# A hybrid decoder block: all eight gate pairs by seven block products, operand sums behind the last head's betas, gate and LayerNorm sums by accumulating transfers

## The chip, the core and the metric

The kernel runs on one core of a Trainium2 chip. The metric is the device time of one execution in microseconds; the time before is the median of three runs.

## What is computed

One layer of a decoder block on a sequence of 1024 tokens with 1024 channels, in float32. The part that matters here, cut from the reference:

```python
mod = c_act @ ada_w[l] + ada_b[l]
sh1, sc1, ga1, sh2, sc2, ga2 = [m[:, None, :] for m in jnp.split(mod, 6, axis=-1)]
h = rmsnorm(x, pre_mix_g[l]) * (1.0 + sc1) + sh1
...
proj = h @ w_in                                   # 1024 -> 1024 (GLU) + 1536 (q, k, v) + 2048 (gates)
glu_in, qkv, gates = jnp.split(proj, [...], axis=-1)
u_val, u_gate = jnp.split(glu_in, 2, axis=-1)
u = causal_depthwise_conv(u_val * jax.nn.sigmoid(u_gate), conv_w, conv_b)   # 512 channels, 31 taps
u = jax.nn.silu(layernorm(u, conv_ln_g, conv_ln_b))
y_conv = u @ w_conv_out
o = stick_breaking_attention(q, k, v)             # 8 heads of 64
y_att = o.reshape(b, s, ATT_WIDTH) @ w_att_out
g_conv, g_att = jnp.split(gates, 2, axis=-1)
merged = jax.nn.sigmoid(g_conv) * y_conv + jax.nn.sigmoid(g_att) * y_att
y = merged @ w_o
x = x + ga1 * rmsnorm(y, post_mix_g[l])
...                                               # then a SwiGLU feed-forward sub-layer of 2816 columns
```

## The kernel before

Channels lie on the 128 partitions and tokens on the free dimension, in two chunks of CH = 512. Each float32 operand of a large product is split into a high and a low part of TensorE's faster float32 form (tiles ending in hi and lo), and a product of 128 x 128 by 128 x 512 is three matmuls: hi by hi, hi by lo, lo by hi. The high part is a copy on ACT (line 143), the low part a subtraction on DVE (line 446 in the gate part, line 153 for whole weights).

The program runs in stages: the norm of x with its modulation (to about 67 us), then attention in four pairs of heads, with GLU and convolution as filler for TensorE, then the gates, the LayerNorm of the convolution, the projections of the two branches (pyc for the convolution, pya for attention), w_o (pwo), the feed-forward part and the final sums. The order of instructions on each engine is set by a scheduler at build time, from priorities, dependencies and how many buffers a tile name has; each engine then runs its own list in order and waits by semaphores. `load` issues a DMA on SP's queue, `store` on POOL's, and a few are issued on ACT's.

In attention a head's `be` tiles (betas) are multiplied on DVE (line 623), transposed by TensorE (`tr`), split into `ahi`/`alo` or, on the diagonal, `dhi`/`dlo` (lines 642 and 643), and multiplied with v (`av`). `pcv` are the products of the convolution, whose weights `cvw` come through SP's queue.

The 2048 gate columns are 16 tiles, taken as 8 pairs. For a pair in `GPAIRS`, the 2 x 2 block product of its weights with h is made from seven block products of 12 matmuls each instead of eight. Two of them (`early`, operands B11 and B21, results in the PSUM tile k, stored to e_d0 and s_d) run ahead, while the other operands aren't there yet; the weights for them are `ew`, split into `a`. The other five (`other_five`) use sums T1 to T4 of blocks of h, made from stored rows of x (`f`, from xm_d) for j = 0 to 3, and sums s1 to s4 of the weight blocks (`gs`), and leave their results in two PSUM tiles, ka and kc. `ga`, `gv`, `gw` are the tiles in which a pair's results are summed on DVE; after a sigmoid they are stored to s_d by POOL. The pairs not in `GPAIRS` (with NPL = 1 it is pair 7) are plain products: `gemm` into the tile pg, 96 matmuls for the pair.

`ln_all` is the LayerNorm of the convolution's four channel tiles `cr`: for each chunk the sum over the four is made in `la`, summed over partitions by a matmul with ones (`lnm`), subtracted, squared, summed again (`lnv`), and turned into a factor (`rstd_from`, lines 135 to 139) with which each `cr` is multiplied (line 851). The two chunks share the tiles `la` and `lm`. Then each `cr` gets gain, bias and swish (line 868), is split, and feeds pyc.

Of the kernel before, what the change touches and what calls it, by code (L numbers as in the profile page):

```python
# [17 lines left out]
P = 128  # L18
D = 1024
# [18 lines left out]
LATER = 100000  # L38
NPL = 1
GORDER = (0, 1, 2, 3, 4, 5, 6, 7)  # L40
# [29 lines left out]
def tile_block(ctx: ExitStack, tc: tile.TileContext, xT, vecs, ada1, ada2, win, wv, wcv, wat, wo, w1, w2, cvw, out):  # L70
# [378 lines left out]
    def prod0(bank_, w, b, first=True):  # L449
        for j in range(HK):  # L450
# [7 lines left out]
            for s, (st, mv) in enumerate(((0, 0), (0, 1), (1, 0))):  # L458
                pe.matmul(bank_, w[st][:, cols], mvs[mv], start=(first and j == 0 and s == 0),  # L459
                          stop=(j == HK - 1 and s == 2), skip_group_check=not first)  # L460

    with ExitStack() as sC:
        pc = mkpool(sC, "pc")
        with ExitStack() as sA:
            pa = mkpool(sA, "pa")
            psz = mkpool(sA, "psz", 2, space=PSUM)
            pst = mkpool(sA, "pst", 2, space=PSUM)
            ident = pa.tile([P, P], F32, name="ident")
# [10 lines left out]
            ndiag = count()  # L479

            def glu(ct):
# [99 lines left out]
            def head(p, hh, qst, kst, klo, vts, oT):  # L581
# [6 lines left out]
                for ci, c in enumerate(order):  # L588
# [5 lines left out]
                    for sc in range(nsc - 1, -1, -1):  # L594
                        probs = []
                        for i in (2 * c, 2 * c + 1):
# [26 lines left out]
                            dve.tensor_tensor(beta[:, :m], beta[:, :m], kap[:, s_lo + 1:s_lo + 1 + m], op=ALU.mult)  # L623
                            probs.append(beta)
# [30 lines left out]
            def attend(p, qk, vts):  # L655
                qs, ks, kl = qk
                oT = pa.tile([P, T], F32, tag="oT", name=f"oT{p}", bufs=1)
                nxt = None
                for hh in range(2):
                    with tc.high_priority(offset=SOONER):  # L660
                        head(p, hh, qs[hh], ks[hh], kl[hh], vts, oT)
                    if hh == 0 and p < 3:
                        nxt = qk_pair(p + 1)
                with tc.high_priority(offset=SOONER):
                    load(o_d[p], oT)
                return nxt
# [7 lines left out]
            for p in range(4):  # L674
# [5 lines left out]
                qk = attend(p, qk, v)  # L680
            conv(3)
            for n in PLAIN:
                gb = banks2(f"pg{n}")
# [32 lines left out]
    with ExitStack() as sG:  # L716
        pg = mkpool(sG, "pg")
        psg = mkpool(sG, "psg", 4, space=PSUM)

        def ot(name, dt=F32):  # L720
            return pg.tile([P, 2, CH], dt, tag="op", name=name, bufs=16)

# [15 lines left out]

        def make_t(name, src, hi_eng, lo_eng):
            t = ot(name, F32R)  # L740
            copy_to(hi_eng, t[:, 0], src)
            lo_eng.tensor_tensor(t[:, 1], src, t[:, 0], op=ALU.subtract)
            return t

        dsh1 = small.tile([P, HK], F32, name="dsh1")
        dve.tensor_tensor(dsh1, mod[:, HK:KT], mod[:, 0:HK], op=ALU.subtract)
        for j in range(HK):
            if j == 0:
                f = [pg.tile([P, T], F32, tag="f", name=f"f{q}_{j}", bufs=2) for q in range(2)]
                b11, b12, b21, b22 = f[0][:, :CH], f[0][:, CH:], f[1][:, :CH], f[1][:, CH:]  # L750
            else:
                b12, b11, b22, b21 = ((xt, st, xt)[j - 1](f"f{q}_{j}") for q in range(4))
            for b, k, c in ((b12, j, 1), (b11, j, 0), (b22, HK + j, 1), (b21, HK + j, 0)):
                load(b, xm_d[k][:, c * CH:(c + 1) * CH])
            sh, ds = mod[:, HK + j:HK + j + 1], dsh1[:, j:j + 1]
            dve.tensor_tensor(b11, b12, b11, op=ALU.subtract)
            dve.scalar_tensor_tensor(b12, b22, ds, b12, op0=ALU.add, op1=ALU.subtract)
            dve.scalar_tensor_tensor(b22, b22, sh, b11, op0=ALU.add, op1=ALU.subtract)
            dve.scalar_tensor_tensor(b21, b21, sh, b22, op0=ALU.add, op1=ALU.subtract)
            for b, src in (("T2", b22), ("T1", b11), ("T3", b12), ("T4", b21)):  # L760
                B0[b, j] = make_t(f"{b}o_{j}", src, act, dve)

        pairs, p1s, t3_done = {}, {}, []

        def pair_load(i):
# [5 lines left out]
            p1s[i] = xt(f"ga{i}")  # L771
            load(p1s[i], e_d0[i])

        def sig_out(t, n, c):
# [3 lines left out]
        def other_five(i):  # L778
            wg, wu = pairs[i]
            p1 = c21 = p1s[i]  # L780
            a11, a12, a21, a22 = wg[:, :CH], wg[:, CH:], wu[:, :CH], wu[:, CH:]
            s1, s2, s3 = (st(f"g{nm}_{i}") for nm in ("s1", "s2", "s3"))
            v, w_ = xt(f"gv_{i}"), xt(f"gw_{i}")
            dve.tensor_tensor(s1, a21, a22, op=ALU.add)
            dve.tensor_tensor(s2, s1, a11, op=ALU.subtract)
# [36 lines left out]
        def ln_all():  # L822
# [5 lines left out]
            for c in range(NCH):  # L828
                cs = hs[c]
                dve.tensor_tensor(s0_, cr[0][:, cs], cr[1][:, cs], op=ALU.add)  # L830
                for ct in (2, 3):
                    dve.tensor_tensor(s0_, s0_, cr[ct][:, cs], op=ALU.add)
                pm = psg.tile([P, CH], F32, tag="ln", name=f"lnm{c}", bufs=1)
# [42 lines left out]
        def ada2_dots(ins, n):  # L876
            for _ in range(n):
                col = a2.popleft()
                w = pg.tile([P, D], F32, tag="f", name=f"ada2_{col}", bufs=2)
                load(w, ada2[col - 2 * KT])  # L880
                with tc.issue_after(ins.ins):
                    dot_c(w, cb, col)
# [1079 lines left out]
```

## Time and profile before

| | |
|---|---|
| median of 3 runs | 1385.55 us (1385.22 to 1388.72) |
| profiled execution | 1385.58 us, span 1383.8 us, granted clock 1.00 |
| TensorE busy | 1369.8 us, 99% of the span, 6844 records |
| VectorE busy | 1041.5 us, 75%, 1593 instructions |
| ScalarE busy | 655.2 us, 47%, 1163 instructions |
| GpSimd busy | 108.8 us, 8%, 251 instructions |
| plain products of pair 7 (pg) | first at 392.0 us |
| early products (k) | 415.7 to 453.9 us |
| gate stage, first product of the other five | 453.9 us |
| first product with w_conv_out (pyc) | 551.4 us |

Times in a row of the profile are microseconds from the span's start, unless they are marked ns. A row names the line of the code, the engine, the operation, the output and the inputs by the program's names, and shapes. A bracket behind a row gives how long the engine had been idle before it and what ended the wait. Matmuls overlap, so that the time from one start to the next, not the duration of one, is what a matmul costs.

### The profile page before, as it was taken

How to read it: one execution, taken by the hardware profiler on the slowest of the kernel's cores; microseconds unless marked ns; L12 is line 12 of the kernel's file. 1: busy time of each engine (PE TensorE's matmuls, PEld its weight loads, DVE VectorE, ACT ScalarE, POOL GpSimd, SP SyncE). 2: the span in 40 equal slices, each digit the busy share in tenths (PEclk: the TensorE clock that was granted, in tenths of full speed). 3: DMA queues.
4: the chain of work that ended last, by engine and by line, in shares of the span. 5: the costliest groups of instructions: out<-in, count | busy, mean ns of one | idle time of the engine just before them, and what ended most of it. 6: DMA issues, size and time to landing. Idle time of an engine off the chain costs nothing.

```text
span 1383.8 us, 18854 instructions
## 1 busy us (share of the span) xinstructions
PE 1369.8 (99%) x6844; PEld 1154.7 (83%) x6844; DVE 1041.5 (75%) x1593; ACT 655.2 (47%) x1163; POOL 108.8 (8%) x251
## 2 busy tenths in 40 slices
PE   8999999999999999999999999999999999999998
PEld 6898888998988788887887888888888888888887
DVE  7997786675857888777597987778877775884354
ACT  6565564464646547313365543324444443434442
POOL 0100001000000011000012200001111110000002
PEclk9999999999999999999999999999999999999999
DMA  9512051140468547855745544457777779596736
GB/s 379 231 39 69 16 167 47 46 138 31 138 205 295 215 148 276 276 183 166 298 137 193 203 148 171 145 191 249 245 242 252 254 262 385 177 337 221 251 113 122
DMA packets 94941, 265.03 MB, mean 192 GB/s; under 512 B 10048, under 2 KB 21440, under 8 KB 93824
## 3 DMA queue, kind: packets, MB, share of 16 engines
q1 hardware_dynamic: 74080, 201.42, 43.2%
q0 software_dynamic: 17904, 57.42, 11.9%
q10 hardware_dynamic: 2864, 4.98, 1.0%
q8 instruction: 54, 0.88, 0.3%
q14 instruction: 39, 0.32, 0.1%
HBM read 192.74 MB, written 71.04 MB: 191 GB/s over the span
## 4 chain that ended last, share of the span: by engine, by line
PE 82%; DMA 5%; issue 5%; DVE 4%; ACT 2%; POOL 1%; SPq 0%; DVEq 0%; POOLq 0%; ACTq 0%
PE ka L1082 15%; PE kc L1082 8%; PE ka L1629 8%; PE pwo L1000 6%; PE ke L1191 4%; PE pb L1629 4%; PE pgv L164 3%; PE k L459 3%; PE pv L538 3%; PE pgg L164 2%; PE pk L164 2%; DMA ada<-in_ada_dram 2%; PE pcv L517 2%; PE pq L164 2%; PE tr L636 2%
## 5 line engine op out<-in xcount | busy, mean ns | idle before, releaser
L612 ACT ACTIVATE ka<-z 128x128 f32<-128x128 f32 (+2 forms) x96 | 47.2, 494 | 44.4 <-PE z L611 35.2
L1629 PE MATMUL ka<-gt,w2f 128*128 128x512 f32 x264 | 63.4, 389 | 0.0
L618 DVE TENSOR_TENSOR_SCAN ka<-ka,eye 128x128 f32<-128x128 f32 (+1 forms) x64 | 51.4, 815 | 11.9 <-ACT ka L612 11.8
L623 DVE TENSOR_TENSOR be<-be,ka 128x127 f32<-128x127 f32 (+2 forms) x96 | 53.8, 573 | 7.1 <-ACT be L614 2.0
L1629 PEld LDWEIGHTS ka<-gt,w2f 128*128 128x128 f32 x264 | 49.5, 188 | 10.3
L119 DVE SCALAR_TENSOR_TENSOR ada<-ada,cb 128x1024 f32<-128x1024 f32 x32 | 39.1, 1224 | 25.2 <-DMA ada<-in_ada_dram 25.0
L614 ACT ACTIVATE be<-z 128x127 f32<-128x127 f32 (+2 forms) x96 | 47.0, 496 | 6.0 <-PE tr L636 5.8
L636 PE MATMUL tr<-ident,be 128*128 128x128 f32 x288 | 46.5, 272 | 0.4 <-DVE be L623 0.4
L1191 PE MATMUL ke<-b,w_hi 128*128 128x512 f32 x176 | 44.3, 394 | 0.0
L621 DVE TENSOR_TENSOR_SCAN ka<-ka 128x512 f32<-128x512 f32 x32 | 40.6, 1275 | 3.7 <-ACT ka L612 3.6
L517 PE MATMUL pcv<-ph,cvw 128*128 128x128 f32 x320 | 42.9, 275 | 0.0
L642 ACT ACTIVATE ahi<-tr 128x512 fp32r<-128x512 f32 x48 | 28.3, 601 | 27.6 <-PE tr L636 19.4
L517 PEld LDWEIGHTS pcv<-ph,cvw 128*128 128x128 f32 x320 | 40.4, 191 | 0.7
L1191 PEld LDWEIGHTS ke<-b,w_hi 128*128 128x128 f32 x176 | 33.0, 188 | 7.7 <-issue 1.0
L143 ACT ACTIVATE gt<-X 128x512 fp32r<-128x512 f32 x33 | 20.3, 629 | 38.8 <-DVE X L1672 11.2
L643 DVE TENSOR_TENSOR alo<-tr,ahi 128x512 fp32r<-128x512 f32 x48 | 32.1, 685 | 7.9 <-ACT ahi L642 7.6
L636 PEld LDWEIGHTS tr<-ident,be 128*128 128x128 f32 x288 | 34.8, 140 | 3.8 <-PE z L611 0.7
L143 ACT ACTIVATE s1o<-s 128x512 fp32r<-128x512 f32 x22 | 13.8, 629 | 49.4 <-PE ka L1082 42.8
L538 PE MATMUL pv<-wv_hi,hhi 128*128 128x256 f32 x128 | 36.8, 288 | 0.2 <-DVE klo L578 0.2
L538 PE MATMUL pv<-wv_hi,hlo 128*128 128x256 f32 x128 | 36.6, 286 | 0.0
L538 PE MATMUL pv<-wv_lo,hhi 128*128 128x256 f32 x128 | 36.2, 284 | 0.0
L578 DVE TENSOR_TENSOR klo<-pk,kst 64x512 fp32r<-64x512 f32 x32 | 22.0, 689 | 18.7 <-ACT kst L575 18.3
(561 smaller groups left out, 4186.1 us busy)
## 6 DMA issues: line engine op xcount, KB each, us to landing
w_d<-w2o POOLq DMA_DIRECT2D x44, 512.0 KB, 7.4
w2f<-w_d SPq DMA_DIRECT2D x44, 512.0 KB, 4.7
ada<-in_ada_dram SPq DMA_DIRECT2D x32, 512.0 KB, 5.4
w2r<-in_w_dram SPq DMA_DIRECT2D x44, 256.0 KB, 3.8
w1g<-in_w_dram SPq DMA_DIRECT2D x21, 512.0 KB, 3.7
w1u<-in_w_dram SPq DMA_DIRECT2D x21, 512.0 KB, 6.0
cvw<-in_cvw_dram SPq DMA_DIRECT2D x20, 512.0 KB, 3.7
ada_w<-in_ada_dram SPq DMA_DIRECT2D x8, 1024.0 KB, 14.7
```

The costliest lines, as they stand in the source:

```text
L164: pe.matmul(bank, st[:, cols], mv[k][:, c * CH:(c + 1) * CH], start=(i == 0 and s == 0), stop=(i == n - 1 and s == 2))
L517: pe.matmul(cv[:, gi * TM:(gi + 1) * TM], wts[n][:, at:at + P], ph[:, g, SH - 1 - d:SH - 1 - d + TM], start=(d == 0), stop=(d == SH - 1))
L538: pe.matmul(pv[:, :256], st[k][:, tcols], mv[:, wc], start=(k == 0 and i == 0), stop=(k == KT - 1 and i == 2))
L612: act.activation(kap[:, s_lo:s_hi], z[:, zo:zo + w], AF.Sigmoid, bias=0.0, scale=-0.125)
L614: act.activation(beta[:, :m], z[:, zo:zo + m], AF.Sigmoid, bias=0.0, scale=0.125)
L618: dve.tensor_tensor_scan(rev, rev, eye[:, CH - w:][:, ::-1], 0.0, op0=ALU.mult, op1=ALU.add)
L623: dve.tensor_tensor(beta[:, :m], beta[:, :m], kap[:, s_lo + 1:s_lo + 1 + m], op=ALU.mult)
L636: pe.transpose(tr[:, o:o + P], probs[ii][:, jo:jo + P], ident)
L1000: pe.matmul(bank_, st[:, cols], mv[k][:, cs], start=(k == 0 and q == 0), stop=(k == KT - 1 and q == 2))
L1082: pe.matmul(bank_, st[:, cols], t[:, mv], start=(first and j == 0 and s == 0), stop=(j == HK - 1 and s == 2), skip_group_check=not first)
L1191: pe.matmul(kbs[f], wes[f][st][:, cols], t[:, mv], start=(i == 0 and j == 0 and st == 0 and mv == 0), stop=(j == HK - 1 and st == 1), skip ...
L1629: pe.matmul(dst, w[st][:, cols], g[mv], start=first and s == 0, stop=last and s == 2, skip_group_check=more)
```

## The change

1. `NPL = 0`: pair 7 is made by seven products like the others.
2. The operand sums (`t_ops`) of rows j = 0 and 1 are made at the end of attention, in tiles of the pool `pc` whose earlier contents (query, key, GLU and convolution tiles) are dead by then. Their first operation is ordered behind the last head's last multiplication of betas (`probs_at`), for the scheduler only. Rows 2 and 3 come later, as before. For this the pool `pc` lives on through the gate stage, the PSUM pools `psz` and `pst` live as long as `sC`, the T and Y operands get a list of places (`T_AT`, `Y_AT`), the tag "op" has 6 buffers instead of 16, and the later ada loads use the tag "ph".
3. The weight sum s1 = a21 + a22 of each pair is a load followed by an accumulating DMA on POOL's queue, instead of a sum on DVE.
4. The channel sum of the LayerNorm is, for each chunk, a load and three accumulating DMAs on POOL's queue, instead of three sums on DVE.
5. The last pair's attention output is stored by ACT's queue instead of SP's.

```diff
-NPL = 1
+NPL = 0
...
+    def t_ops(j, b11, b12, b21, b22, tiles, behind=None):
+        sh, ds = mod[:, HK + j:HK + j + 1], dsh1[:, j:j + 1]
+        t1 = dve.tensor_tensor(b11, b12, b11, op=ALU.subtract)
+        if behind:
+            tc.add_manual_dep(t1.ins, behind, ...SCHED_ONLY)
+        dve.scalar_tensor_tensor(b12, b22, ds, b12, op0=ALU.add, op1=ALU.subtract)
+        dve.scalar_tensor_tensor(b22, b22, sh, b11, op0=ALU.add, op1=ALU.subtract)
+        dve.scalar_tensor_tensor(b21, b21, sh, b22, op0=ALU.add, op1=ALU.subtract)
+        for b, src in (("T2", b22), ("T1", b11), ("T3", b12), ("T4", b21)):
+            t = tiles(f"{b}o_{j}")
+            copy_to(act, t[:, 0], src)
+            dve.tensor_tensor(t[:, 1], src, t[:, 0], op=ALU.subtract)
+            B0[b, j] = t
...
-                    load(o_d[p], oT)
+                    (act.dma_start if p == 3 else load)(o_d[p], oT)
...
             conv(3)
+            dve.tensor_tensor(dsh1, mod[:, HK:KT], mod[:, 0:HK], op=ALU.subtract)
+            for j, rows, tags in ((0, (("u", 1), ("ph", 2)), (("qst", 3),) * 3 + (("ph", 2),)),
+                                  (1, (("klo", 3),) * 2, (("kst", 3),) * 3 + (("klo", 3),))):
+                f = [pc_tile(f"f{q}_{j}", *rows[q]) for q in range(2)]
+                for q, k in enumerate((j, HK + j)):
+                    load(f[q], xm_d[k].rearrange("p (c n) -> p c n", n=CH))
+                at = iter(tags)
+                t_ops(j, f[0][:, 0], f[0][:, 1], f[1][:, 0], f[1][:, 1], lambda name: pc_tile(name, *next(at), F32R),
+                      probs_at[0])
...
-        for j in range(HK):
-            if j == 0:
-                f = [pg.tile([P, T], F32, tag="f", name=f"f{q}_{j}", bufs=2) for q in range(2)]
...
+        for j in (2, 3):
+            b12, b11, b22, b21 = ((st, xt)[j - 2](f"f{q}_{j}") for q in range(4))
             for b, k, c in ((b12, j, 1), (b11, j, 0), (b22, HK + j, 1), (b21, HK + j, 0)):
                 load(b, xm_d[k][:, c * CH:(c + 1) * CH])
...
             load(p1s[i], e_d0[i])
+            s1s[i] = st(f"gs1_{i}")
+            load(s1s[i], win[21 + 2 * i][:, :CH])
+            nc.gpsimd.dma_start(s1s[i], win[21 + 2 * i][:, CH:], accum_op=ALU.add)
...
-            dve.tensor_tensor(s1, a21, a22, op=ALU.add)
...
-                dve.tensor_tensor(s0_, cr[0][:, cs], cr[1][:, cs], op=ALU.add)
-                for ct in (2, 3):
-                    dve.tensor_tensor(s0_, s0_, cr[ct][:, cs], op=ALU.add)
+                load(s0_, channels(u_d[0])[:, cs])
+                for ct in (1, 2, 3):
+                    nc.gpsimd.dma_start(s0_, channels(u_d[ct])[:, cs], accum_op=ALU.add)
...
-                w = pg.tile([P, D], F32, tag="f", name=f"ada2_{col}", bufs=2)
+                w = flat(pc_tile(f"ada2_{col}", "ph", 2))
```

How the change moves instructions shows at three places. The first is DVE at the end of the last head: `be` are the betas, `ka` the scans ahead of them, `wg_lo` the low parts of pair 7's plain weights, `dlo` and `alo` the low parts that attention waits for, `a` those of the early products' weights, and `f` the rows for the operand sums. Before:

```order
398 L618 SCALAR_TENSOR_TENSOR ka_1_0_4036<-ka_1_0_4036,eye 128x128
399 L623 TENSOR_TENSOR be_1_0_0_4037<-be_1_0_0_4037,ka_1_0_4036 128x127
400 L153 TENSOR_TENSOR wg_lo<-wg_raw,wg_hi 128x1024
401 L618 SCALAR_TENSOR_TENSOR ka_1_1_4046<-ka_1_1_4046,eye 128x256
402 L623 TENSOR_TENSOR be_1_1_0_4047<-be_1_1_0_4047,ka_1_1_4046 128x255
403 L643 TENSOR_TENSOR dlo_625<-tr_1_1_1_4013,dhi_624 128x384
404 L653 TENSOR_TENSOR oT_3595<-av_1_3_3832,oT_3595 64x512
405 L153 TENSOR_TENSOR wg_lo<-wg_raw,wg_hi 128x1024
406 L643 TENSOR_TENSOR alo_1_1_0_4029<-tr_1_1_0_4023,ahi_1_1_0_4028 128x512
```

The same place now:

```order
400 L644 TENSOR_TENSOR be_1_0_0_4038<-be_1_0_0_4038,ka_1_0_4037 128x127
401 L644 TENSOR_TENSOR be_1_1_0_4048<-be_1_1_0_4048,ka_1_1_4047 128x255
402 L467 TENSOR_TENSOR f_0_4138<-f_0_4138 128x512
403 L467 TENSOR_TENSOR f_1_4158<-f_1_4158 128x512
404 L446 TENSOR_TENSOR a_0_4181<-ew_4178,a_0_4181 128x512
405 L446 TENSOR_TENSOR a_0_4220<-ew_4178,a_0_4220 128x512
406 L471 SCALAR_TENSOR_TENSOR f_0_4138<-f_0_4139,dsh_607,f_0_4138 128x512
407 L471 SCALAR_TENSOR_TENSOR f_1_4158<-f_1_4159,dsh_607,f_1_4158 128x512
408 L675 TENSOR_TENSOR oT_3596<-av_1_3_3833,oT_3596 64x512
409 L665 TENSOR_TENSOR dlo_626<-tr_1_1_1_4014,dhi_625 128x384
410 L446 TENSOR_TENSOR a_1_4202<-ew_4199,a_1_4202 128x512
411 L472 SCALAR_TENSOR_TENSOR f_0_4139<-f_0_4139,mod,f_0_4138 128x512
```

The two wg_lo are gone, and sums of rows 0 and 1 and casts of the first early weights stand between the betas and dlo.

The second place is POOL's queue in the gate stage. Before, it held the stores of the gates alone:

```order
96 L617 MEMSET be_1_1_0_4047 128x1
97 L101 DMA s_d_80<-gw_4656 128x512
98 L101 DMA s_d_79<-gv_4655 128x512
99 L101 DMA s_d_80<-ga_4644 128x512
100 L101 DMA s_d_82<-gw_4759 128x512
```

Now the accumulating transfers of the gate sums (gs) and of the LayerNorm (la) stand among them; these are the rows with the second chunk's la:

```order
115 L795 DMA gs_6_5184<-in_win_dram 128x512
116 L101 DMA s_d_86<-gw_4982 128x512
117 L854 DMA la<-u_d_75 128x512
118 L101 DMA s_d_85<-gv_4981 128x512
119 L854 DMA la<-u_d_76 128x512
120 L795 DMA gs_7_5288<-in_win_dram 128x512
121 L101 DMA s_d_86<-ga_4769 128x512
122 L854 DMA la<-u_d_77 128x512
```

The three la transfers, each of which waits for the landing of the one before, have stores and gate sums between them.

The third is SP's queue while the convolution of the third channel tile runs (cvw are its weights). Before:

```order
66 L98 DMA cvw_3_3570<-in_cvw_dram 128x1024
67 L98 DMA cvw_4_3580<-in_cvw_dram 128x1024
68 L98 DMA u_d_76<-co_0_3532 128x4x128
69 L98 DMA cvw_0_4074<-in_cvw_dram 128x1024
70 L98 DMA cvw_1_4084<-in_cvw_dram 128x1024
```

Now:

```order
67 L98 DMA cvw_3_3571<-in_cvw_dram 128x1024
68 L98 DMA f_0_4138<-xm_d_103 128x1024
69 L98 DMA f_1_4159<-xm_d_108 128x1024
70 L98 DMA cvw_4_3581<-in_cvw_dram 128x1024
71 L98 DMA u_d_76<-co_0_3533 128x4x128
```

Two loads of 512 KB for the rows 0 and 1 stand ahead of cvw_4. On TensorE the 96 matmuls of pg between attention's last products are gone, k has 24 more and ka and kc 60 more; between the second chunk's lnv and the first pyc stand 71 matmuls, before 140.

More of the change, by code (lines that the diff above doesn't have):

```diff
@@ L460, in prod0, with pc_tile @@
                           stop=(j == HK - 1 and s == 2), skip_group_check=not first)
+    pc = mkpool(sS, "pc")
+    dsh1 = small.tile([P, HK], F32, name="dsh1")
+    def t_ops(j, b11, b12, b21, b22, tiles, behind=None):
+        sh, ds = mod[:, HK + j:HK + j + 1], dsh1[:, j:j + 1]
+        t1 = dve.tensor_tensor(b11, b12, b11, op=ALU.subtract)
+        if behind:
+            tc.add_manual_dep(t1.ins, behind, mybir.DependencyInfo(
+                mybir.DependencyClass.NoSync, mybir.DependencyReason.SCHED_ONLY))
+        dve.scalar_tensor_tensor(b12, b22, ds, b12, op0=ALU.add, op1=ALU.subtract)
[6 more added lines that the diff above has]
+            B0[b, j] = t
+    def pc_tile(name, tag, bufs, dt=F32):
+        return pc.tile([P, 2, CH], dt, tag=tag, name=name, bufs=bufs)
     with ExitStack() as sC:
-        pc = mkpool(sC, "pc")
+        psz = mkpool(sC, "psz", 2, space=PSUM)
+        pst = mkpool(sC, "pst", 2, space=PSUM)
         with ExitStack() as sA:
             pa = mkpool(sA, "pa")
-            psz = mkpool(sA, "psz", 2, space=PSUM)
-            pst = mkpool(sA, "pst", 2, space=PSUM)
             ident = pa.tile([P, P], F32, name="ident")
@@ L479, in tile_block @@
             ndiag = count()
+            probs_at = [None]
             def glu(ct):
@@ L622, in head @@
                                                        op1=ALU.bypass)
-                            dve.tensor_tensor(beta[:, :m], beta[:, :m], kap[:, s_lo + 1:s_lo + 1 + m], op=ALU.mult)
+                            probs_at[0] = dve.tensor_tensor(beta[:, :m], beta[:, :m], kap[:, s_lo + 1:s_lo + 1 + m],
+                                                            op=ALU.mult).ins.name
                             probs.append(beta)
@@ L718, in tile_block @@
         psg = mkpool(sG, "psg", 4, space=PSUM)
+        T_AT = [("klo", 3)] * 2 + [None] * 6
+        Y_AT = [("u", 1)] + [("qst", 3), ("kst", 3)] * 3 + [None] * 6 + [("klo", 3)] * 3
+        slots = iter(T_AT + Y_AT)
         def ot(name, dt=F32):
-            return pg.tile([P, 2, CH], dt, tag="op", name=name, bufs=16)
+            at = next(slots)
+            if at:
+                return pc_tile(name, *at, dt)
+            return pg.tile([P, 2, CH], dt, tag="op", name=name, bufs=6)
         def xt(name):
@@ L737, in flat @@
             return t.rearrange("p a b -> p (a b)")
[L739 to L746, printed above, removed]
-        for j in range(HK):
-            if j == 0:
-                f = [pg.tile([P, T], F32, tag="f", name=f"f{q}_{j}", bufs=2) for q in range(2)]
-                b11, b12, b21, b22 = f[0][:, :CH], f[0][:, CH:], f[1][:, :CH], f[1][:, CH:]
-            else:
-                b12, b11, b22, b21 = ((xt, st, xt)[j - 1](f"f{q}_{j}") for q in range(4))
+        for j in (2, 3):
+            b12, b11, b22, b21 = ((st, xt)[j - 2](f"f{q}_{j}") for q in range(4))
             for b, k, c in ((b12, j, 1), (b11, j, 0), (b22, HK + j, 1), (b21, HK + j, 0)):
                 load(b, xm_d[k][:, c * CH:(c + 1) * CH])
[L755 to L763, printed above, removed]
+            t_ops(j, b11, b12, b21, b22, lambda name: ot(name, F32R))
+        pairs, p1s, s1s, t3_done = {}, {}, {}, []
         def pair_load(i):
@@ L781, in other_five @@
             a11, a12, a21, a22 = wg[:, :CH], wg[:, CH:], wu[:, :CH], wu[:, CH:]
-            s1, s2, s3 = (st(f"g{nm}_{i}") for nm in ("s1", "s2", "s3"))
+            s1, (s2, s3) = s1s[i], (st(f"g{nm}_{i}") for nm in ("s2", "s3"))
             v, w_ = xt(f"gv_{i}"), xt(f"gw_{i}")
-            dve.tensor_tensor(s1, a21, a22, op=ALU.add)
             dve.tensor_tensor(s2, s1, a11, op=ALU.subtract)
```

## The prediction

> **What bounds the kernel now.** I read the page's busy line and slices first, then the table by stage around the gates, then the tiles of the products that are exchanged, and last the timelines of the places where TensorE waits.
>
> The page: busy time by engine, then TensorE's slices and granted clock.
>
> ```profile
> PE 1369.8 (99%) x6844; PEld 1154.7 (83%) x6844; DVE 1041.5 (75%) x1593; ACT 655.2 (47%) x1163; POOL 108.8 (8%) x251
> ...
> PE   8999999999999999999999999999999999999998
> ...
> PEclk9999999999999999999999999999999999999999
> ...
> PE 82%; DMA 5%; issue 5%; DVE 4%; ACT 2%; POOL 1%; SPq 0%; DVEq 0%; POOLq 0%; ACTq 0%
> ```
>
> TensorE is busy 99% of the span at full clock, and carries 82% of the chain that ended last. The table by stage covers the end of attention, the gates and the convolution branch (busy us and counts of PE, weight loads, DVE, ACT, POOL; then clock, DMA share, GB/s).
>
> ```profile
> core 0: us, PE busy (x) PEld busy (x) DVE busy (x) ACT busy (x) POOL busy (x), PEclk, DMA share, GB/s
> ...
> 400.00:450.00 50.00, 50.00 (x223) 41.27 (x222) 29.96 (x47) 24.88 (x46) 0.00 (x0) 1.00 0.80 274
> 450.00:500.00 50.00, 49.13 (x213) 39.65 (x212) 42.65 (x71) 23.73 (x39) 3.82 (x7) 1.00 0.53 189
> 500.00:550.00 50.00, 49.95 (x217) 40.30 (x216) 46.39 (x68) 33.16 (x48) 5.41 (x10) 1.00 0.65 229
> ```
>
> Only 450 to 500 holds 0.87 us without a matmul. VectorE is second, 93% busy in 500 to 550, POOL nearly empty. So a matmul taken out pays its full pitch, work moved off DVE pays nothing unless PE waited for it, and every new wait counts against TensorE's order. A profiled execution of 1385.58 (span 1383.8) is the base; the median of the runs is 1385.55, so no correction is needed. A measurement tells a difference from none at about 0.3%, 4.2 us.
>
> **The products.** Tile k holds the early products, pg the plain products of pair 7.
>
> ```profile
> L164 PE MATMUL pg<-hhi,wg_hi x32: 389/389/478, 392.0 to 414.8; 128*128 128x512 f32 x32
> ...
> L459 PE MATMUL k<-hhi,a x112: 389/389/405, 415.7 to 453.6; 128*128 128x512 f32 x112
> ...
> L459 PE MATMUL k<-hlo,a x56: 389/389/398, 416.0 to 453.4; 128*128 128x512 f32 x56
> ```
>
> The 168 matmuls of k start at 415.7 and the next product at 453.87 (below): 38.1 / 168 = 0.227 us each; the 0.389 of a row overlaps its neighbours. Pair 7 needed 3 x 32 = 96 in pg and now needs 7 products of 12, 24 of them in k and 60 in the gate stage: 84. Gain 12 x 0.227 = 2.72 us, on the path, since nothing else runs there. The gate stage starts (96 - 24) x 0.227 = 16.3 us earlier, at 437.5 instead of 453.87; below I count from this start, G.
>
> **The stall at the head of the gate stage.** PE's timeline, then DVE's (start, duration, idle before and what ended it).
>
> ```profile
> 453.87 0.61 PE L459 MATMUL kc<-T1o,s1o 128*128 128x512 f32 x2
> ...
> 457.95 1.52 PE L459 MATMUL kc<-T1o,s1o 128*128 128x512 f32 x6
> 460.34 2.97 PE L459 MATMUL ka<-T3o,s3o 128*128 128x512 f32 x12 [0.87 <-DVE gv L792]
> ```
>
> ```profile
> 458.78 0.69 DVE L832 TENSOR_TENSOR la<-la,cr 128x512 f32<-128x512 f32 x1 [2.30 <-DMA cr<-u_d]
> 459.50 0.69 DVE L792 TENSOR_TENSOR gv<-ka,ga 128x512 f32<-128x512 f32 x1
> ```
>
> Six matmuls from 457.95 end their pitch at 459.31; the next starts at 460.34, 1.03 us late. It waited for gv, which frees its bank, and gv stood on DVE behind a LayerNorm sum that waited 2.30 us for its load. These six sums leave DVE, so the stall goes: -1.03 us. What is late next there is nothing I can name: rows 2 and 3 of operand sums need 16 operations of about 0.6 us, 10 us, after loads that follow the early weights, against some 20 us left until G.
>
> **The tail of the last head.** DVE now has 13 T operations of rows 0 and 1 between the last betas and the casts that attention and the early products wait for.
>
> ```profile
> 390.58 1.22 DVE L153 TENSOR_TENSOR wg_lo<-wg_raw,wg_hi 128x1024 fp32r<-128x1024 f32 x1 [0.76 <-ACT wg_hi L143]
> 391.73 0.68 DVE L618 TENSOR_TENSOR_SCAN ka<-ka,eye 128x256 f32<-128x256 f32 x1
> 392.51 0.43 DVE L623 TENSOR_TENSOR be<-be,ka 128x255 f32<-128x255 f32 x1
> 392.86 0.55 DVE L643 TENSOR_TENSOR dlo<-tr,dhi 128x384 fp32r<-128x384 f32 x1
> ```
>
> Out go two wg_lo of 1.22 and the wait of 0.76; in come f, f (0.6 each), a, a, f, f ahead of dlo. I walk the new order at 0.60 us an operation and 0.66 where it takes three operands: the betas end near 391.4, the first a at 392.6, dlo at 395.6. The old PE order, with k in pg's place, wants them at 392.5 and 395.5; the others have 1 to 5 us in hand. I put +0.3 (0 to +1.5, if each of the first casts is one operation later).
>
> SP: the f loads of rows 0 and 1, 512 KB each, now stand ahead of a conv weight, and an ada load that waits for DVE stands ahead of two early weights.
>
> ```profile
> 361.16 2.47 SPq L98 DMA_DIRECT2D cvw<-in_cvw_dram  x2
> ...
> cvw<-in_cvw_dram SPq DMA_DIRECT2D x20, 512.0 KB, 3.7
> ...
> ew<-in_win_dram SPq DMA_DIRECT2D x7, 512.0 KB, 4.7
> ```
>
> The second of that cvw pair was issued at 363.30, after a wait, and used from about 369.4. Behind two more loads, sharing the engines with them, it lands near 370.2, while its first matmul, moved behind a score pair, is due at about 369.95: +0.2 (0 to +1.5). The ada load waits for the last T operand of row 0, near 405; ew then lands near 410.5, its cast ends near 412, its product is due at 414: nothing, with 2 us cover. Together, tail and SP: +0.5 (0 to +3).
>
> **Gate sums by accumulating transfers.** Seven DVE sums go, eight loads and eight accumulating DMAs on POOL come. Nearest rows: issue to landing, in us. "out_dram<-yc" is the only accumulating one; L1797 are its eight issues with the engine's time for each.
>
> ```profile
> out_dram<-yc POOLq DMA_DIRECT2D x4, 512.0 KB, 8.4
> ...
> out_dram<-y POOLq DMA_DIRECT2D x16, 256.0 KB, 2.7
> ...
> sga<-s_d SPq DMA_DIRECT2D x16, 256.0 KB, 3.9
> ...
> s_d<-gw POOLq DMA_DIRECT2D x7, 256.0 KB, 3.7
> ```
>
> ```profile
> out_dram<-yc POOLq DMA_DIRECT2D x4, 256.0 KB, 7.4
> ...
> L1797 POOL DMA_DIRECT2D out_dram<-yc x8: 1189/1234/2747, 1354.0 to 1365.7; - x8
> ...
> DMA to landing us min/median/max: 5.9/7.8/10.3
> ```
>
> Lower end: a plain 256 KB transfer by POOL in this stage takes 3.7, and an accumulating one is issued in 1.23 us, against 0.54 for a plain one: 4.4. Upper end: 7.4, the median of the same size, though those were issued back to back and queue. One of twice the bytes at the queue's front took 5.9. I take 4.9, nearer the lower end, because here each goes alone. Pair 0's sum is the tightest: its load lands near 425, its accumulation near 430, and its cast is due near 435. Later pairs have tens of us. Cost: nothing.
>
> [...]
>
> **LayerNorm sums by accumulating transfers.** Each of the two chunks is now a load and three accumulations, each waiting for the one before, in POOL's queue among the gate stores. LayerNorm's own matmuls (mean, then variance):
>
> ```profile
> L834 PE MATMUL lnm<-la,ones x4: 590/590/591, 463.2 to 501.9; 128*128 128x512 f32 x4
> ...
> L847 PE MATMUL lnv<-la,ones x4: 590/590/591, 475.8 to 519.5; 128*128 128x512 f32 x4
> ```
>
> By counting matmuls in the new order: lnm of chunk 0 is 168 after G (38.1 us), lnv of chunk 0 at 217 (49.2), lnm of chunk 1 at 325 (73.7, with the second passes of two earlier ones 74.2), lnv of chunk 1 at 401, the first pyc at 472. Chunk 0's load stands behind the four cr loads on SP and its accumulations are third, sixth and tenth of POOL's gate work; I put its end near G+28: no cost, 10 us cover.
>
> Chunk 1 reuses the tile. Its load waits for the last of the four multiplies of chunk 0:
>
> ```profile
> 483.38 2.49 DVE L851 TENSOR_TENSOR cr<-cr,la 128x512 f32<-128x512 f32 x4
> ```
>
> That ended 10.05 us after lnv's start at 475.8, with four foreign operations of 0.6 between; the new order has none there, so 7.6: G+56.8. Load 3.9 (as sga): 60.7. Three accumulations of 4.9: 75.4, against 74.2: PE waits +1.2 us. With 4.4 each it is 73.9, no wait; with 7.4, 82.9, +8.7. What queues behind a waiting accumulation are gate stores, whose readers come some 100 us later.
>
> **LayerNorm to the convolution's projection.** Between the last lnv and the first pyc stood 140 matmuls, 31.8 us; now 71, 16.1 us.
>
> ```profile
> 533.21 2.15 DVE L868 TENSOR_TENSOR lm<-cr,la 128x1024 f32<-128x1024 f32 x1
> ...
> 551.44 0.39 PE L819 MATMUL pyc<-hhi,wc_hi 128*128 128x512 f32 x1
> ```
>
> Before, this first product tile was ready about 17 us after lnv (519.03 to 536). In the new order seven operations fewer stand between, 4.2 us: 13 against 16. The next tiles come 7 us apart and I count 1.5 to 3.5 us in hand: +0.3 (0 to +2). Stores by ACT's queue, PSUM pools that live longer, and the later ada loads cost nothing that TensorE sees: their readers are tens of us behind.
>
> **Sum.** -2.72 - 1.03 + 0.5 + 1.2 + 0.3 = -1.75: 1385.58 - 1.75 = 1383.8.
>
> **Rivals.**
> *All cover holds.* An accumulation alone needs 4.5 us or less and the tail's casts fit: -3.75, 1381.8. For it: POOL is idle for most of the stage. Against: hand-counted margins of 0 to 3 us at four places, not all of which can be expected to hold.
> *The accumulations are late (the other side).* Place: lnm of chunk 1. At 7.4 each PE waits 8.7 us: -3.75 + 0.8 + 8.7 = +5.75, 1391.3. It starts to cost above 4.5 us each, cancels the gain at 5.5 ((74.2 + 2.95 - 60.7) / 3), and is slower than a measurement can miss at 6.9. For it: the only rows of this kind, 7.4 and 8.4, and POOL's stores take 3.7 beside a busy DVE against 2.7 late in the kernel. Against: those accumulations queue behind each other, and 5.9 was enough for twice the bytes. [...]
> *The tail of the last head stalls.* DVE's 13 operations or SP's loads hold conv and the early products 3 to 4 us: -3.75 + 1.5 + 3.5 = +1.25, 1386.8. For it: margins near zero at dlo and cvw; against: PE has conv matmuls that wait for neither DVE nor those loads.
>
> **Chances.** Forecast 0.40, all cover 0.30, late accumulations 0.14, tail 0.16. Faster by over 0.3% needs below 1381.4: 0.4 us more than all cover, which two short hiccups in the gate stage could give; I count 0.13 of the 0.30. Slower needs 1389.8: the late accumulations and a 0.02 of the tail combined with them, 0.16. Same 0.71. Range: 1381.0 (all cover and 0.8 more) to 1390.0 (accumulations at about 7). It leaves out about 0.15.
>
> **What will show it.** The pg group is gone, k has 192 matmuls, G lies near 437.5 to 438.5. If G is later by more than 1.5 us, the tail stalled; its row is a PE wait for an a or dlo cast or for cvw. The 0.87 wait for gv is gone. The la accumulations' issue to landing decides the rest: 4.4 to 5.5 us is my case, with a PE wait of 0 to 3 us at the second lnm, ended by a DMA or POOL; above 6 us the rival. A wait at pyc for a cast of ACT or DVE would show the fifth term. I am wrong if a wait appears in the gate stage behind POOL's queue, or after 600, where I expect the old order.

## The result and the profile after

The changed kernel took 1392.99 us in the median of 5 runs, the kernel before 1385.37: ratio 1.0051, interval [1.0038, 1.0064]. It is slower by 7.6 us; 1383.8 was forecast, and the range ended at 1390.0. The profiled execution took 1391.6 (span 1389.8), the fastest of the five. In the ratios of this document one execution of one later kernel is left out: it took 1961 us, at a mean granted clock of 0.655.

The page after shows busy times and TensorE's slices almost unchanged. The table by stage, which before held 0.87 us without a matmul in 450 to 500 and 0.05 in 500 to 550, now reads:

```profile
400.00:450.00 50.00, 49.17 (x221) 40.48 (x220) 35.06 (x55) 26.94 (x50) 4.02 (x5) 1.00 0.93 330
450.00:500.00 50.00, 49.58 (x215) 39.91 (x214) 37.39 (x60) 24.25 (x38) 10.67 (x17) 1.00 0.76 217
500.00:550.00 50.00, 45.18 (x183) 35.71 (x182) 32.72 (x52) 23.01 (x35) 8.58 (x14) 0.93 0.62 180
```

In 500 to 550 TensorE lacks 4.8 us, and its granted clock, 1.00 before, is 0.93. From 400 to 450 the transfers are at 0.93 of the engines' time, before at 0.80. The view of waits for TensorE, 385 to 560 us (total, times, longest):

```profile
PE lnm L856 <- DMA la<-u_d: 4.8, 1, 4.8
PE ka L459 <- ACT s2o L143: 0.8, 1, 0.8
PE lnv L869 <- DVE la L867: 0.4, 1, 0.4
```

The wait for gv is gone, another of like size stands there, for pair 1's s2o, and the second lnm waits for the last accumulation of la. A view of waits gives the idle time; from start to start a wait of a product costs about 0.16 more (0.389 of a matmul's row less its pitch of 0.227). PE's timeline at that place, and the table in stretches of 2 to 5 us:

```profile
509.73 2.47 PE L459 MATMUL ka<-T4o,a 128*128 128x512 f32 x10
517.01 2.07 PE L856 MATMUL lnm<-la,ones 128*128 128x512 f32 x2 [4.82 <-DMA la<-u_d]
518.10 1.84 PE L459 MATMUL ka<-T4o,a 128*128 128x512 f32 x2
519.74 0.63 PE L459 MATMUL ka<-T2o,s2o 128*128 128x512 f32 x1
520.17 3.77 PE L459 MATMUL kc<-T1o,s1o 128*128 128x512 f32 x10
```

```profile
512.00:517.00 5.00, 0.20 (x1) 0.00 (x0) 0.00 (x0) 0.00 (x0) 0.61 (x2) 0.92 0.89 238
517.00:519.00 2.00, 1.99 (x3) 0.95 (x4) 0.00 (x0) 0.00 (x0) 0.00 (x0) 0.50 0.10 39
519.00:521.00 2.00, 2.00 (x6) 1.54 (x5) 1.02 (x2) 1.56 (x3) 0.00 (x0) 0.50 0.54 131
521.00:523.00 2.00, 2.00 (x6) 1.59 (x5) 2.00 (x5) 1.34 (x3) 0.55 (x1) 0.50 0.00 0
523.00:525.00 2.00, 2.00 (x10) 1.62 (x10) 2.00 (x5) 1.02 (x2) 0.00 (x0) 1.00 0.34 131
```

The wait costs 4.98 us from start to start. The clock is granted at 0.50 from 516.2 to 523.0 (the 0.92 of 512 to 517 is 0.8 us at half clock), and the ten matmuls of 520.17 take 3.6 us instead of 2.3: of these 6.8 us 6.0 lie behind the wait, and 3.0 us are lost. The chain that was late, on POOL's timeline, with the view of its line:

```profile
499.62 0.86 POOL L854 DMA_DIRECT2D la<-u_d  x1 [1.26 <-DMA la<-u_d]
505.75 0.87 POOL L854 DMA_DIRECT2D la<-u_d  x1 [4.71 <-DMA la<-u_d]
510.63 0.86 POOL L854 DMA_DIRECT2D la<-u_d  x1 [2.04 <-DMA la<-u_d]
```

```profile
L854 POOL DMA_DIRECT2D la<-u_d x6: 842/855/871, 447.2 to 510.6; - x6
...
DMA to landing us min/median/max: 4.4/5.8/7.4
```

**Where the 6 us between the two profiled executions come from.** Tile pya starts at 603.7, before at 597.7:

```profile
L164 PE MATMUL pya<-ohi,wa_hi x64: 389/389/389, 603.7 to 646.1; 128*128 128x512 f32 x64
```

This +6.0 is -2.7 (12 matmuls), +5.0 (the wait), +3.0 (half clock), and +0.7 of small differences, among them 0.2 from stages before 392 and 0.6 from the wait at lnv; the s2o wait replaces the gv wait. At the last of the early feed-forward products (ke) it is +4.9, since the wait of 0.9 at pwo near 648 is gone here, and at the end of the program +6.0 again, 0.6 of it a wait for uw.

### The profile page after: what moved, and what is told of

Same layout as the page of the kernel before. It is cut to its first block, busy times and chain, and to the rows that moved or that the text cites. A ratio compares the mean times of both kernels' runs of the same rounds, so it can differ in the third digit from the quotient of the medians.

```text
span 1389.8 us, 18884 instructions
## 1 busy us (share of the span) xinstructions
PE 1370.6 (99%) x6832; PEld 1154.0 (83%) x6832; DVE 1041.0 (75%) x1593; ACT 658.5 (47%) x1169; POOL 122.9 (9%) x268
## 3 DMA queue, kind: packets, MB, share of 16 engines
q10 hardware_dynamic: 2720, 4.98, 0.9%
## 4 chain that ended last, share of the span: by engine, by line
PE 85%; DMA 7%; DVE 4%; issue 1%; ACT 1%; SPq 0%; ACTq 0%; DVEq 0%; POOLq 0%
PE ka L1104 12%; PE ka L1651 8%; PE kc L1104 7%; PE pwo L1022 6%; PE ke L1213 4%; PE pb L1651 4%; PE pgv L164 3%; PE pya L164 3%; PE pyc L841 3%; PE pv L559 3%; PE ka L459 3%; PE k L459 3%; PE pgg L164 2%; PE pk L164 2%; PE pcv L538 2%; PE pq L164 2%
## 5 line engine op out<-in xcount | busy, mean ns | idle before, releaser
L1651 PEld LDWEIGHTS ka<-gt,w2f 128*128 128x128 f32 x264 | 49.6, 188 | 10.3
L459 PE MATMUL k<-hhi,a 128*128 128x512 f32 x128 | 40.4, 391 | 0.0
L1637 DVE TENSOR_TENSOR gt<-X,gt 128x512 fp32r<-128x512 f32 x33 | 22.4, 690 | 18.8 <-ACT gt L143 18.7
```

What stands on the lines that cost most here:

```text
L1651: pe.matmul(dst, w[st][:, cols], g[mv], start=first and s == 0, stop=last and s == 2, skip_group_check=more)
```

## The experiments

Times are medians and ratios to the kernel before on the same chip; its medians there were 1385.3 to 1386.4. The theory at first: the accumulation chain of LayerNorm's second chunk makes TensorE wait and leaves it at half clock. The rival: the rest of the change, above all its traffic at the start of the gate stage, is what costs. Each kernel has one profiled execution, three have two, and the waits told are those of that execution; where it lies far from the median of its runs, the text says so.

**LayerNorm sums on DVE again** (in the changed kernel).

```diff
-                load(s0_, channels(u_d[0])[:, cs])
-                for ct in (1, 2, 3):
-                    nc.gpsimd.dma_start(s0_, channels(u_d[ct])[:, cs], accum_op=ALU.add)
+                dve.tensor_tensor(s0_, cr[0][:, cs], cr[1][:, cs], op=ALU.add)
+                for ct in (2, 3):
+                    dve.tensor_tensor(s0_, s0_, cr[ct][:, cs], op=ALU.add)
```

> The changed kernel with the LayerNorm channel sums made on DVE again, all else kept. Theory (the accumulation chain of chunk 1 holds TensorE 5.0 us at the second lnm and leaves it at half clock for another 3.4 us): both go, no row of half clock after the start, 1383 to 1385 us, the same as before or up to 2 us faster; a wait of about 1 us for gv may come back. Rival (the operand sums in the tail, the gate sums and the larger DMA traffic cost the time, and the lnm wait only shows it): 1388 us or more, with the wait at another place of the gate stage.

1388.52 us, 1.0018 [1.0010, 1.0027]. The wait at lnm went, but the time fell by 4.5 us, not by 8: the time is the rival's. In the profiled execution (1390.2, near the slow end of its runs) the wait for gv came back with 2.4 us and 3.4 us at half clock, 1.7 lost, behind it. A wait of 2.2 us, with another 3.4 us at half clock behind it, appeared in the seam near 1180 us, where the feed-forward part goes over from its first products (uw) to its second (gb):

```profile
1181.27 0.50 PE L1651 MATMUL ka<-gb,wa 128*128 128x512 f32 x1 [2.17 <-ACT gb L143]
```

**Gate sums on DVE too, and seven products alone.** Two kernels without any accumulating sum: the changed one with both kinds on DVE, and the one before with `NPL = 0` as its only edit.

> The changed kernel with the gate sums and the LayerNorm sums on DVE again: seven products for all pairs and the operand sums in dead tiles remain. Theory: 12 matmuls fewer and no chain, 1382 to 1384 us. Rival (the tail of the last head or the DMA traffic in 400 to 450 costs several us): 1386 us or more.

> The kernel before with seven products for pair 7 alone; operand sums, gate sums and LayerNorm sums stay where they were. Theory: 12 matmuls at 0.227 us fewer, 2.7 us, less up to 2 us for DVE work that comes closer to the gate stage: 1382.5 to 1385 us. Rival (operand sums made only after the tail come too late, since the gate stage starts 16 us earlier): 1390 us or more, with a PE wait for a T tile at the start of the gate stage.

1390.72 us, 1.0031 [1.0019, 1.0043], and 1390.95 us, 1.0040 [1.0025, 1.0056]. Both expectations of the theory failed, and the rivals' times came: 12 matmuls fewer make the kernel slower by themselves. Waits of TensorE in 350 to 660 with seven products alone:

```profile
PE ka L459 <- DVE s2o L446: 1.4, 1, 1.4
PE k L459 <- ACT ee L706: 1.0, 1, 1.0
PE k L459 <- DVE a L446: 1.0, 1, 1.0
PE ka L459 <- DVE gv L792: 0.9, 1, 0.9
PE k L459 <- ACT a L143: 0.6, 1, 0.6
PE kc L459 <- ACT s1o L143: 0.5, 1, 0.5
```

None is large. Together they are 5.4 us, where the kernel before waits 1.8 in the same stretch, and pya starts 4.2 us later than before. The plain products of pair 7, whose weights need no early start, had given DVE, ACT and the transfers 16 us ahead of the gate stage: with seven products alone DVE is busy without a break from 425 to 435 us (before 8.6 of these 10), and the transfers of 400 to 450 take 0.96 of their engines' time (before 0.80). Which of the three is short isn't shown: with both sums on DVE and rows 0 and 1 made early the transfers stand at 0.81, and TensorE still waits 2.8 us, for two s1o and a gv.

**A tile of its own for chunk 1's sum**, so that its chain can start early.

```diff
+            own = pc_tile("lnown", "u", 1)[:, 0]
...
+                sum_ = own if c else s0_
```

> The changed kernel with a tile of its own (in the dead place of u) for chunk 1's channel sum, so that its load and three accumulations need not wait for chunk 0's multiplies; the number of accumulating DMAs stays. Theory (the wait comes from when the chain may start, then from its three serial landings): the chain starts some 40 us earlier, ends near G+48 where the second lnm is due at G+51.7, PE waits 0 to 2 us there and at the first lnm, 1382 to 1386 us. Rival (the accumulating DMAs as such, by POOL's queue or the traffic, are the cost): 1389 us or more, with stores or gate sums late.

1394.15 us, 1.0065 [1.0051, 1.0079]: a miss. The lnm wait went, but the chain now ran at 400 to 430, among the loads for the gate stage; the gate sums' accumulations were issued at 435.9 instead of 428.0, and TensorE waited 4.7 us for the first s1o, with 4.4 us at half clock behind it, and 1.6 for a gw at 471. The wait had been moved.

**Holding the cr loads back.** cr (four loads of 512 KB) stands on SP among the weights of pairs 0 and 1. The edit puts the loads behind pair 1's second weight, for the scheduler only: in the kernel with both sums on DVE, and in the kernel before. In these two the first DVE sum and the first lnm are also put behind the T3 product of pair 1, so that the whole LayerNorm comes later.

```diff
+                cl = load(cr[ct], channels(u_d[ct]))
+                tc.add_manual_dep(cl.ins, gw_ld[1], ...SCHED_ONLY)
```

> Seven products for all pairs and the operand sums in dead tiles, gate and LayerNorm sums on DVE, and in addition the four 512 KB loads of cr held back on SP behind the weights of pairs 0 and 1, with the first LayerNorm sum behind the T3 product of pair 1. Theory (the start of the gate stage, 16 us earlier, is late for its transfers: cr and the gate weights share the DMA engines): the waits of 1.7 for s1o and 1.0 for gv at 437 to 447 shrink to under 1 us together, 1384 to 1387 us. Rival (what is lost lies in the seam after 1150 or in the tail of attention, not in the loads): no change against the kernel without the held loads, 1389 to 1391 us.

> The kernel before with the same edit alone: cr loads behind the weights of pairs 0 and 1, first LayerNorm sum behind the T3 product of pair 1. Theory: the 1.03 us wait for gv at 460 goes and nothing else comes, 1384.5 us, 0.07% faster, inside what a measurement can tell. Rival (the shorter way from the last lnv to pyc, 71 matmuls instead of 140, makes pyc wait): 1387 us or more with a PE wait at pyc.

1390.54 us, 1.0033 [1.0021, 1.0044], and 1390.73 us, 1.0038 [1.0025, 1.0051]. Neither did what the theory said. In the first a wait of 2.7 for s2o stayed, and waits of 2.4 for gb in the seam near 1180, with half clock behind; its time is the rival's. In the second pyc waited 1.8 us and a gv 1.6; the wait at pyc and the time are as its rival had them.

**Pair 7 plain, the rest of the change kept; and one accumulation more or less for chunk 1** (one more adds a tile twice, one instead of three leaves two tiles out of the mean).

> The changed kernel with pair 7 by plain products again, all else kept. Theory (the accumulation chain costs by its own length, about 30 us from the first lnv to the second lnm, and the new order has 100 matmuls, 22.7 us, there): a wait of about 7 us at the second lnm, half clock for 3 to 4 us behind it, no wait at the start of the gate stage: 1393 to 1397 us. Rival (the earlier start of the gate stage, through pair 7, makes the chain late): 1389 us or less.

> The changed kernel with a fourth accumulation for chunk 1 (the last channel tile is added twice, so its mean is another). The scheduler puts the second lnm 12 matmuls (2.7 us) later. Theory: the wait there grows by one landing, 5.8, less 2.7, from 5.0 to about 8 us, and the half clock behind it stays at 6 to 7 us of time, 3.4 us lost: about 1395 us. Rival (the loss of clock grows with the wait): half clock for 10 us, 1397 us or more.

> The changed kernel with one accumulation instead of three for chunk 1 (two channel tiles are left out of its mean). The scheduler puts the second lnm at 288 instead of 325 matmuls. Theory: chain G+61.2 + 3.3 + 5.8 = 70.3 against 65.3 and some 2.7 of small waits: PE waits about 2.3 us, and less than 2 us are lost by half clock: 1386 to 1388 us. Rival (the wait isn't set by the number of landings): a wait near 5 us and 1391 us.

1409.74 us, 1.0172 [1.0158, 1.0185]; single executions of 1394.86 and 1395.14. The first missed both its theory and its rival by over 12 us: beside 3.3 us at the second lnm, TensorE waited 3.8 at an lnv, 6.2 at pyc and 1.6 and 1.2 at two other places, and was three times at half clock for 3.4 us; it says little about the chain. With one accumulation more the wait at lnm was 6.8 (8 expected) and the time as forecast. Its stretches show that the longer wait didn't lengthen the time at half clock, again 6.8 us, of which more now lies in the wait itself:

```profile
521.00:523.00 2.00, 0.00 (x0) 0.00 (x0) 0.00 (x0) 0.00 (x0) 0.00 (x0) 0.50 0.98 282
523.00:525.00 2.00, 1.97 (x3) 0.94 (x4) 0.00 (x0) 0.00 (x0) 0.00 (x0) 0.50 0.28 90
525.00:527.00 2.00, 2.00 (x6) 1.56 (x5) 1.43 (x3) 1.22 (x3) 0.00 (x0) 0.50 0.34 109
527.00:529.00 2.00, 2.00 (x10) 1.61 (x9) 2.00 (x4) 1.73 (x3) 0.00 (x0) 0.96 0.00 0
```

With one accumulation the wait was 2.6 (2.3 forecast), but the time 7 us above the forecast, through a wait of 2.3 for s1o, small ones from 650 to 1190, and 3.4 us at half clock both behind the lnm and in the seam. The scheduler brings the second lnm forward as the chain gets shorter, so that shortening it removes less than it should.

**Each of the two accumulating parts alone**: LayerNorm by DMA in the kernel before, and in the changed kernel the gate sums on DVE.

> The kernel before with the LayerNorm sums alone by accumulating DMAs. The order has the first lnm 84 matmuls (19 us) after the start of the gate stage and 108 (24.5 us) from the first lnv to the second lnm. Theory: the chain needs some 27 us for chunk 0 and 30 us for chunk 1, so PE waits about 8 and 5 us, each with about 3.4 us of half clock behind it, less 1 us for the gv wait: 1395 to 1406 us. Rival (with less other traffic the accumulations land in under 4.9 us): at most 1390 us.

> The changed kernel with the gate sums alone on DVE again. The order has the first lnm 84 and the second 103 matmuls (23.4 us) after the first lnv. Theory (the LayerNorm chain is long by itself): accumulations still land in 5 to 6 us each, PE waits about 10 us at the first lnm and 6 at the second, 1398 to 1408 us. Rival (the eight gate sums on POOL's queue and their traffic make the LayerNorm accumulations slow): landings under 5 us each, 1390 us or less.

1393.61 us, 1.0059 [1.0044, 1.0075], and 1396.01 us, 1.0065 [1.0048, 1.0082]. LayerNorm by DMA alone costs 8 us, with no other edit: waits of 2.4 and 2.1 at the two lnm, 3.4 us at half clock behind the second, and 2.1 for an hhi. Its size was over-estimated, since accumulations landed in 3.6 to 6.4 us there. In the second kernel too the time came out below the theory's range. Without the gate sums' transfers they landed in 3.7 to 6.2, mean 5.1 against 5.7 and 5.4 in the two traces of the changed kernel, and two waits of 3 us remain. The gate sums add little to the landings, and are not the cause.

**Chunk 1 on DVE, chunk 0 by DMA**, all else as changed.

> The changed kernel with the second chunk's LayerNorm sum on DVE again, the first chunk's and the gate sums still by accumulating DMAs. The first lnm and lnv stand where they stood (168 and 217 matmuls after the start of the gate stage), the second lnm at 293. Theory: the wait of 5.0 us at the second lnm and the 3.4 us of half clock behind it go, nothing comes at the start of the gate stage: 8.4 us below the changed kernel up to the projections, 1383 to 1385 us, or up to 1387 if the seam near 1180 loses more. Rival (the transfers as such, not this chain): 1389 us or more.

1389.32 us, 1.0021 [1.0011, 1.0030]. The profiled execution (1387.2) has no wait at lnm and no half clock; pya starts at 596.5, 1.1 us earlier than before, though the stages before 392 ended 1.2 us later: up to there 2.3 us of the gain are there. They are lost again in small waits, and the median, 2 us above the theory's range, is the rival's; the profiled execution is near the fast end of its runs (1385.8 to 1392.9). Its waits:

```profile
PE ka L459 <- ACT s2o L143: 1.3, 1, 1.3
PE pwo L1027 <- ACT mhi L966: 1.0, 1, 1.0
PE ka L1109 <- DVE uw L1528: 0.6, 1, 0.6
PE pwo L1027 <- DVE mlo L833: 0.5, 1, 0.5
PE ka L1656 <- ACT gb L143: 0.4, 1, 0.4
```

**The same with the cr loads held back.**

> The changed kernel with the second chunk's LayerNorm sum on DVE, and in addition the cr loads held behind the weights of pairs 0 and 1 on SP. Theory (cr shares the transfers with pair 1's weights, which pair 1's s2o waits for): the wait of 1.5 us at 444 goes, 1385 to 1388 us in the median, 1 to 2 us below the kernel without the held loads. Rival (what is lost lies behind 640 and differs from run to run): the same median within 1 us, about 1389 us.

1383.9 us, 0.9988 [0.9979, 0.9997]: better than expected, and the only kernel that beats the one before, by 0.1%. Its waits after 350 us, and pya's start:

```profile
PE ka L1111 <- DVE uw L1530: 0.7, 1, 0.7
PE ka L1658 <- ACT gb L143: 0.4, 1, 0.4
PE ka L1111 <- DVE T_2o L1235: 0.3, 1, 0.3
PE ka L1658 <- DVE gb L1644: 0.3, 1, 0.3
PE lnm L863 <- DMA la<-u_d: 0.2, 1, 0.2
```

```profile
L164 PE MATMUL pya<-ohi,wa_hi x64: 389/389/389, 595.4 to 637.8; 128*128 128x512 f32 x64
```

No wait is left between 392 and 660 but 0.2 at the first lnm, whose chain landed just in time. The load of gw1a, which pair 1's s2o had waited for, landed after 7.1 us, against 10.0 without the held loads, as the theory had it. Against the first trace without the held loads (1387.2) the span is 3.0 us shorter, but only 0.5 of it lies between 392 and pya, where the s2o wait is gone; 0.7 lies ahead and 1.9 behind, and what makes these isn't shown.

**The held loads with the chain as changed.**

> The changed kernel with nothing but the cr loads held behind the weights of pairs 0 and 1; both LayerNorm chunks by accumulating DMAs. The second lnm stands at 321 matmuls. Theory (two independent losses): the waits at 437 to 446 go, the wait at the second lnm stays at 4 to 7 us with 3 to 7 us at half clock behind it: about 1388 to 1391 us, 2 to 4 us below the changed kernel and 5 to 7 above the kernel with chunk 1 on DVE and held cr loads (1383.9). Rival (the late transfers also make the chain late): the wait at lnm falls below 2 us and the time to 1385 or less.

1393.31 us, 1.0047 [1.0032, 1.0062].

```profile
PE lnm L858 <- DMA la<-u_d: 6.3, 1, 6.3
PE pyc L842 <- ACT hhi L894: 1.4, 1, 1.4
PE k L459 <- DVE a L446: 0.7, 1, 0.7
```

The waits at 437 to 446 went (a k waits 0.7 at 429), and the time didn't fall: slower than expected, the lnm wait took more, and the half clock lasted 10.2 us, longer than with the wait of 6.8 above. This kernel and the one ahead of it differ in the sum of chunk 1 alone. The medians lie 9.4 us apart; they were taken on two chips, and against the kernel before on the same chip the difference is 8.2. With the same loads, the profiled executions put it to about 6 us of waiting, some 3 lost at half clock, and a wait of 1.4 at pyc behind them. This trace (1395.9) is near the slow end of its runs, so that these three add up to more than the medians show.

**Three kernels once more**, for a second trace.

> The kernel with the second chunk's sum on DVE once more, for a second trace. Theory: the same waits up to the projections; where this execution is slower than the first (1387.2 us), the difference lies at waits for transfers (444, or the seam near 1180 to 1190). Rival: it is spread over the whole span as a lower clock or longer matmuls.

> The changed kernel once more. Theory: again a wait of 4 to 6 us at the second lnm with 6 to 7 us at half clock behind it, landings of the chain at 5 to 6.5 us, 1391 to 1394 us. Rival: a wait at another place of like size.

> The kernel before once more, for the spread of its waits: the same waits at 460 and 648 and less than 0.5 us at the seam, 1385 to 1386 us. If the seam near 1180 waits a microsecond or more here too, it is not the change that makes it wait.

1391.48, 1390.12 and 1386.93 us. The changed kernel again waited at the second lnm (3.7 us, landings of 4.7, 6.3 and 3.9, then half clock), and this time 1.6 for s1o; its time is 0.9 us below the range expected. Against the second trace of the kernel before, pya starts 5.6 us later (6.0 in the first pair). The kernel with chunk 1 on DVE waited 2.7 us for s1o at 438, where its first execution had waited 1.3 for s2o at 446, and fell to half clock there: the start of the gate stage waits in both, but for another transfer, first a load of pair 1's weights, then pair 0's accumulation. Even the kernel before waits in the seam in this execution:

```profile
PE ka L1082 <- DVE uw L1501: 0.9, 1, 0.9
PE ka L1629 <- ACT gb L143: 0.8, 1, 0.8
PE ka L459 <- DVE gv L792: 0.8, 1, 0.8
```

So waits for uw and gb of 0.9 and 0.8, absent in its first trace, come without the change. Waits for gb of 1.3 to 2.8 with half clock behind stand only in traces of kernels with seven products for all pairs (four of them); whether the change lengthens them is open.

## Why the prediction was wrong, point by point

**The products.** The count is right. k has 192 matmuls, the gate stage's first product of pair 0 stands at 435.0 with 12 of k behind it (437.5 was forecast for the end of k, 438.2 was measured), and where no wait came the gain arrived: with chunk 1 on DVE and the cr loads held, pya starts 2.3 us earlier than before, 2.8 against the same start. But "on the path, since nothing else runs there" left out what the plain products gave time for: as the only edit, seven products for pair 7 made the kernel 5 us slower.

**The stall at the head of the gate stage.** The step said that what is late next "is nothing I can name". In the first trace it was s2o of pair 1 (0.8 us), whose weight gw1a took 10 us to land; in the second s1o of pair 0 (1.6), whose accumulation landed at 436.8. The wait changed its name, and -1.03 became about 0. With chunk 0's sum by DMA and the cr loads held it was gone, with chunk 1 on DVE or by DMA; with both sums on DVE a wait of 2.7 for s2o stayed in spite of the held loads.

**The tail of the last head and SP.** +0.5 was put; +0.2 came in the first pair of traces, +0.6 in the second. The hand-walked margins held.

**Gate sums by accumulating transfers.** "Cost: nothing" was too good. Pair 0's accumulation landed at 433.2 (430 was forecast, 435 was due), pair 1's took 8.4 us, and in three other executions, where pair 0's landed at 436.8 to 438.0, s1o is late by 1.6 to 2.7. That the transfers of this stage would take 0.93 of the engines' time, instead of 0.80, was left out of the estimate.

**LayerNorm sums.** This is the step that failed, by its size: +1.2 was put, 8.0 came. The place and the mechanism were forecast: a chain that lands late at the second lnm. Of the chain's working, the load took 2.8 us to land (3.9), the three accumulations 5.8, 4.4 and 6.3 with 0.8 between them, 17.4 in all (14.7), and the multiplies of chunk 0 ended 4.4 us later than I had them (61.2 after the start instead of 56.8), partly because TensorE itself was 2.6 later. 4.9 as the duration of one was wrong by 0.6 on the average. All this makes 5.0 of wait. The other 3.0 are the half clock, of which the prediction said nothing: every wait in it was priced at its own length. That the chain makes this loss is shown three times: with LayerNorm on DVE the wait goes, in the kernel before LayerNorm by DMA alone costs 8 us, and with the same loads chunk 1's chain alone costs 8. The whole 7.6 us aren't the chain's alone, though, since with LayerNorm on DVE the kernel stays 2.6 us slower than the one before, in its trace at the start of the gate stage and in the seam.

The rival on the other side was this mechanism at this place, and had 0.14. It needed 6.9 us for each accumulation to be slower than a measurement can miss; with the half clock and without the small gains, 5.5 on the average were enough. With that term, the forecast's own 1.2 would have changed little (idle times of 1.3, 1.5 and 1.6 us, with chunk 1 on DVE, with both sums on DVE and in the changed kernel's second trace, had no half clock; one of 1.6, with pair 7 plain, had), but the middle of its bounds (a wait of 4 us) would have been about 7 with the 3.0 lost here, and the chance of a slower kernel higher.

**LayerNorm to pyc.** +0.3 was put, no wait came here; 1.4 and 1.5 came in the kernels with held cr loads and with one accumulation more, whose lnm waited longer, 1.8 in the kernel before with a later LayerNorm, and 6.2 with pair 7 plain.

**After 600.** The old order was expected. The waits behind 600 add up to 1.4 and 2.3 us in the two traces of the kernel before, to 1.1 and 0.3 in those of the changed one, and to 0.3 to 4.0 over all kernels. What decides this is open; no run tells it.

## What to carry to other kernels

Work that covers nothing visible may still cover transfers and casts: before TensorE work is taken out, ask which loads must land by the new, earlier time, and add up what else moves then. A sum moved from an engine that has room to a chain of dependent transfers becomes as long as its landings (here three times 4 to 7 us), and must be started that much earlier. All seven waits of TensorE of 3.4 to 7.0 us between 430 and 550 us came with half clock here, and six of fourteen of 2.2 to 3.2 us: price such a wait at its length plus what the half clock behind it loses, 1.4 to 3.1 us here.

## What the runs showed of the hardware

In these traces TensorE's granted clock fell to 0.50 in or behind some of its waits and stayed there for 3.4 us, 6.8 us (changed kernel, both traces, and with a tile of its own and with one accumulation more) or, once, 10.2 us (changed kernel with held cr loads), never a time between, the end of a program apart (from 1383.6 of 1383.8 us in the kernel before): all are one, two or three times 3.41 us (the 6.83 of the changed kernel are two). All seven waits of 3.4 to 7.0 us, counted from start to start, that these traces hold between 430 and 550 us had it. Of fourteen waits of 2.2 to 3.2 us behind 392 us six had it and eight had not (2.56 at 446 in the kernel with LayerNorm on DVE had, 3.15 at 504 in the one with gate sums on DVE had not). One of 1.7 had it too (at 437, pair 7 plain), and so had two pairs of short ones in the seam (idle for 1.5 and 0.9 us at 1182, cr held and both sums on DVE; 1.3 and 0.3 at 1186, one accumulation). So waits of like length fared differently, and what decides it isn't shown.

An accumulating DMA of 256 KB from POOL's queue into la landed after 3.6 to 7.8 us, a median of 5.8 in the changed kernel, with 0.85 us to issue (1.23 in the rows before); those into gs took 3.9 to 8.4 in the changed kernel, and in the tile of its own, among the loads of 400 to 430, the first took 10.3. Stores of the same size beside them took 4.8 to 5.2 us in the median, before 3.7 to 3.9.
